# Scan layer: the B, C and x tiles of groups 1 to 3 projected with 512-column matmuls and a later sum

## The chip, the cores and the metric

The kernel runs on one core of a Trainium2 chip. A core has a matrix engine (TensorE, "PE" in the profile, with "PEld" for its weight loads), a vector engine (VectorE, "DVE"), an activation engine (ScalarE, "ACT"), GpSimd ("POOL") and SyncE ("SP"), which here only issues weight loads. The engines run side by side; each takes its own instructions strictly in the order in which the program wrote them, and waits for others through semaphores. Matmul results land in PSUM, a small memory of eight banks of 128 x 512 fp32 values; everything else is in SBUF.

The metric is the device time of one execution, in microseconds (us). Lower is better.

## What is computed

A trunk of two layers on 256 tokens of 1024 features. Each layer is a gated feed-forward block, a token mixer, and another feed-forward block, each followed by a layer norm. The mixer of layer 0 is a sparse attention, that of layer 1 a Mamba-2 scan. The change is in the scan only:

```python
def ssd_mixer(x, w_in, conv_w, conv_b, ...):
    z, xbc, dt = jnp.split(x @ w_in, [SSM_INNER, SSM_INNER + SSM_CONV_DIM], axis=-1)
    conv = conv_b + xbc_pad[:, 0:seq] * conv_w[0]          # 4 taps along the tokens
    for k in range(1, SSM_CONV):
        conv = conv + xbc_pad[:, k:k + seq] * conv_w[k]
    xs, b_in, c_in = jnp.split(jax.nn.silu(conv), ...)
    ...                                                    # dt, decay, chunked scan of 2 x 128 tokens
    yz = y.reshape(...) * jax.nn.silu(z)                   # gate, norm per group, norm_g
    return yz @ w_out
```

There are 4 groups of 512 channels of x (and of z), and one B and one C tile of 128 channels for each group.

## The kernel before

**Products in three parts.** fp32 accuracy is reached by splitting each weight tile and each activation into a high half H and a low half L; a product is H·H + H·L + L·H, three matmuls (`mm3`, L555 to L557). The weights stream in as *units* of 128 x 1024 values. SyncE loads a unit ("raw"), ScalarE casts it to its high half (`make`, L349, tile `wh`), VectorE subtracts to get the low half (`lows`, L378, tile `wl`). For six units of the scan (`by_dma`) ScalarE writes the negated high half (L355) and a GpSimd DMA adds the raw values (L356) instead. There are ten slots of `wh`/`wl`; `W.pump(n)` first does the low halves that are due, then casts up to n further units into slots that have come free.

**Projection of a B, C or x tile.** `proj_b` (L703) takes one weight unit, 128 output channels, and multiplies it with both halves of the transposed activations `xT`. The tile `xT.HL` holds, for each of 8 slices of the features, 256 columns of high halves and then 256 columns of low halves. Per slice there are three matmuls of 256 columns, 24 for a tile. `proj_w` (L712), used by the feed-forward blocks, does the same sum in another form: 8 matmuls of H with all 512 columns of `xT.HL` into a whole PSUM bank, then 8 matmuls of L with the 256 high columns, added to the first half of the bank. The two halves of the bank then have to be added: in the feed-forward blocks ScalarE copies one half out (L962) and VectorE adds the other (L963).

**The convolution.** `conv` (L1550) takes a projected tile in PSUM: ScalarE makes tap 3 and the bias (L1552), VectorE adds the three other taps (L1555), each on top of the one before, and the SiLU on ScalarE (L1547) is put off to the next tile (`late`, `flush`).

**Order of the scan's front.** Eight `bc_tile`s (four of B, four of C), with `cumsums` (sums of dt·a, needed by the decay; from there a 32 KB DMA to `scr` and the loads `decay_load` on the GpSimd queue) after tile 5; then the four x tiles of group 0, with the products C·B of all groups (`cb`, `cb_cross`, L1581 and L1573) after the second; then z of group 1, and the transposes `x_tok` of group 0. Each tile's projection goes to one of three PSUM banks in turn (`xbank`, tile `pxs`).

**The loop over groups.** For group g the list `f` holds eight pieces of TensorE work that fill the gaps of the scan's chain: for g = 0 and 1 the four x tiles of group g + 1 and four half tiles of z (`z_half`); for g = 2 the x tiles of group 3 between pieces of the output projection. Between the pieces stand, in this order: `f[0]`, `x_tok`, `f[1]`, `f[2]`, `diag(0)` and `gate(0)`, `f[3]`, `square(0)`/`root(0)`, `carry`, `diag(1)`, `gate(1)`, `norm(0)`, `f[4]`, `square(1)`/`root(1)`, `decay_seg`, `f[5]`, `y_tr(0)` (L1666), `norm(1)` (L1661), `f[6]`, `y_tr(1)`, `decay_exp`, `f[7]`. `gate` is VectorE (L1649, L1650), `square` ScalarE (L1654), `root` VectorE (L1657) and a GpSimd power (L547), `norm` ScalarE, and `y_tr` needs `norm`.

## Time and profile before

| | us |
|---|---|
| median of 3 runs | 1013.47 (1013.46 to 1014.56) |
| the profiled execution | 1013.54 |
| its span, from first to last instruction | 1011.8 |

The profile is of one execution; the span leaves 1.7 us of its time outside. The views used are: the page (busy time of each engine; the chain of work that ended last), the table of stretches (per stretch: its length, then busy us and count for PE, PEld, DVE, ACT and POOL, then granted clock of TensorE, share of the DMA engines, GB/s), the groups of instructions by line and shape (`xcount | busy us, mean ns of one | idle before`), the waits (who waited for whom: us in total, times, longest) and the timeline (start, duration, engine, line, operation, output<-inputs, form, xcount, and in brackets the idle time before and what ended it). Instructions in a row overlap at their ends, so the cost of one in a queue is the distance from its start to the start of the next.

### The profile page before, as it was taken

How to read it: one execution, taken by the hardware profiler on the slowest of the kernel's cores; microseconds unless marked ns; L12 is line 12 of the kernel's file. 1: busy time of each engine (PE TensorE's matmuls, PEld its weight loads, DVE VectorE, ACT ScalarE, POOL GpSimd, SP SyncE). 2: the span in 40 equal slices, each digit the busy share in tenths (PEclk: the TensorE clock that was granted, in tenths of full speed). 3: DMA queues.
4: the chain of work that ended last, by engine and by line, in shares of the span. 5: the costliest groups of instructions: out<-in, count | busy, mean ns of one | idle time of the engine just before them, and what ended most of it. 6: DMA issues, size and time to landing. Idle time of an engine off the chain costs nothing.

```text
span 1011.8 us, 14601 instructions
## 1 busy us (share of the span) xinstructions
PE 1000.9 (99%) x5279; PEld 847.7 (84%) x5279; DVE 913.8 (90%) x1294; ACT 657.8 (65%) x950; POOL 106.1 (10%) x153
## 2 busy tenths in 40 slices
PE   9999999999999999999999999999999999999996
PEld 7888888898788888888888888999889888888885
DVE  6999998789799999988999997787899899999985
ACT  6676775476657676754767675486876546776670
POOL 0101110200001110000111000151110101010000
PEclk9999999999999999999999999999999999999999
DMA  9979899352547999792899978347875554999751
GB/s 341 283 241 299 291 259 345 121 171 81 199 135 203 263 295 266 260 336 83 222 252 294 274 251 306 132 148 229 226 229 201 194 212 120 296 293 292 204 189 42
DMA packets 64664, 229.60 MB, mean 227 GB/s; under 512 B 7280, under 2 KB 8112, under 8 KB 64592
## 3 DMA queue, kind: packets, MB, share of 16 engines
q1 hardware_dynamic: 52128, 183.95, 50.8%
q0 software_dynamic: 12464, 44.72, 21.8%
q8 instruction: 41, 0.67, 0.3%
q14 instruction: 31, 0.25, 0.1%
HBM read 193.48 MB, written 1.08 MB: 192 GB/s over the span
## 4 chain that ended last, share of the span: by engine, by line
PE 95%; POOL 1%; DVE 1%; ACT 1%; DMA 1%; SPq 0%; issue 0%; DVEq 0%; POOLq 0%
PE pmm L557 13%; PE pmm L556 13%; PE pmm L555 13%; PE acc L555 10%; PE acc L556 10%; PE acc L557 10%; PE ptr L556 3%; PE ptr L557 3%; PE ptr L555 3%; PE pmm L717 2%; PE ptr L820 1%; PE ptr L1638 1%; PE pxs L555 1%; PE pxs L556 1%; PE pxs L557 1%; PE ptr L717 1%
## 5 line engine op out<-in xcount | busy, mean ns | idle before, releaser
L349 ACT CAST wh<-raw 128x1024 fp32r<-128x1024 f32 (+2 forms) x431 | 429.6, 1043 | 117.5 <-DVE raw L316 80.7
L378 DVE TENSOR_TENSOR wl<-raw,wh 128x1024 fp32r<-128x1024 f32 x421 | 493.3, 1212 | 11.1 <-ACT wh L349 11.1
L555 PE MATMUL acc<-wh,hH 128*128 128x512 f32 (+1 forms) x352 | 137.9, 392 | 0.0
L556 PE MATMUL acc<-wl,hH 128*128 128x512 f32 (+1 forms) x352 | 136.6, 388 | 0.0
L557 PE MATMUL acc<-wh,hL 128*128 128x512 f32 (+1 forms) x352 | 136.6, 388 | 0.0
L555 PE MATMUL pmm<-wh,xT 128*128 128x512 f32 (+2 forms) x320 | 126.0, 394 | 0.1
L556 PE MATMUL pmm<-wl,xT 128*128 128x512 f32 (+2 forms) x320 | 123.6, 386 | 0.4 <-DVE wl L378 0.4
L557 PE MATMUL pmm<-wh,xT 128*128 128x512 f32 (+2 forms) x320 | 123.5, 386 | 0.0
L289 POOL DMA_DIRECT2D raw<-raw x59 | 50.7, 866 | 401.7 <-DVE raw L316 216.5
L555 PE MATMUL pmm<-wh,xf 128*128 128x512 f32 x224 | 87.9, 392 | 0.0
L557 PE MATMUL pmm<-wh,xf 128*128 128x512 f32 x224 | 87.3, 390 | 0.0
L556 PE MATMUL pmm<-wl,xf 128*128 128x512 f32 x224 | 87.2, 389 | 0.0
L316 DVE TENSOR_TENSOR raw<-raw,raw 128x1024 f32<-128x1024 f32 x69 | 82.8, 1218 | 0.4
L557 PEld LDWEIGHTS acc<-wh,hL 128*128 128x128 f32 x352 | 66.1, 188 | 13.6
L556 PEld LDWEIGHTS acc<-wl,hH 128*128 128x128 f32 x352 | 66.2, 188 | 13.4 <-DVE wl L378 0.5
L555 PEld LDWEIGHTS acc<-wh,hH 128*128 128x128 f32 x352 | 66.2, 188 | 12.8
L556 PEld LDWEIGHTS pmm<-wl,xT 128*128 128x128 f32 x320 | 60.5, 189 | 12.9 <-DVE wl L378 1.5
L557 PEld LDWEIGHTS pmm<-wh,xT 128*128 128x128 f32 x320 | 60.2, 188 | 12.8 <-DVE xT L552 1.0
L555 PEld LDWEIGHTS pmm<-wh,xT 128*128 128x128 f32 x320 | 60.4, 189 | 11.1 <-ACT wh L349 0.5
L557 PEld LDWEIGHTS pmm<-wh,xf 128*128 128x128 f32 x224 | 42.0, 188 | 8.8
L555 PEld LDWEIGHTS pmm<-wh,xf 128*128 128x128 f32 x224 | 42.0, 188 | 8.6
L556 PEld LDWEIGHTS pmm<-wl,xf 128*128 128x128 f32 x224 | 42.1, 188 | 8.5
(332 smaller groups left out, 1821.3 us busy)
## 6 DMA issues: line engine op xcount, KB each, us to landing
raw<-in_wts_dram SPq DMA_DIRECT2D x338, 512.0 KB, 5.4
raw<-raw POOLq DMA_DIRECT2D x59, 512.0 KB, 6.1
M<-scr POOLq DMA_DIRECT2D x8, 512.0 KB, 6.2
lng<-in_ln_g_dram POOLq DMA_DIRECT2D x6, 512.0 KB, 6.3
lnb<-in_ln_b_dram POOLq DMA_DIRECT2D x6, 512.0 KB, 5.1
wl<-raw POOLq DMA_DIRECT2D x6, 512.0 KB, 5.9
raw<-in_wts_dram SPq DMA_DIRECT2D x4, 408.0 KB, 7.6
raw<-in_wts_dram SPq DMA_DIRECT2D x4, 256.0 KB, 3.9
```

Of the source, the lines that this page charges most:

```text
L289: self.nc.gpsimd.dma_start(self.raw[r], self.raw[other], accum_op=ALU.add)
L316: self.nc.vector.tensor_add(self.raw[r], self.raw[r], self.raw[other])
L349: nc.scalar.copy(h[:, c:c + n], raw[:, c:c + n])
L378: self.nc.vector.tensor_sub(lo[:, s], raw[:, s], h[:, s].bitcast(F32))
L555: nc.tensor.matmul(ps, lh, rh, start=first, stop=False, skip_group_check=on)
L556: nc.tensor.matmul(ps, lh, rl, start=False, stop=False, skip_group_check=on)
L557: nc.tensor.matmul(ps, ll, rh, start=False, stop=last, skip_group_check=on)
L717: nc.tensor.matmul(ps, H[:, k * 128:(k + 1) * 128], xT.HL[:, k, :], start=k == 0, stop=False)
L820: nc.tensor.transpose(pt[:, i * 256 + t * 128:i * 256 + (t + 1) * 128], h[:, i * 128:(i + 1) * 128], ident)
L1638: nc.tensor.matmul(py[:, h * 64:(h + 1) * 64], m[:, h * 128:(h + 1) * 128], y[t][:, h * 64:(h + 1) * 64], start=True, stop=True)
```

## The change

The B and C tiles and the x tiles of groups 0 to 2 (the title counts them 1 to 3) no longer go through `proj_b` and `conv` but through a new `conv_tile`; the x tiles of group 3 stay. That is 8 + 12 = 20 tiles.

```diff
-    def proj_w(ps, xT, u):
+    def proj_w(ps, xT, u, retire=True):
...
+        halves, taps = [], []
+        def conv_sum():
+            for ps, v, i, out_t in halves:
+                a = f1("cv")
+                nc.vector.tensor_add(v, ps[:, :SEQ], v)
+                nc.scalar.activation(a, v, AF.Identity, bias=convp_sb[:, 4, i:i + 1], scale=convp_sb[:, 3, i:i + 1])
+                taps.append((v, a, i, out_t))
+            halves.clear()
+            flush()
+        def conv_taps():
+            for v, a, i, out_t in taps:
+                for s in range(1, 4):
+                    nc.vector.scalar_tensor_tensor(a[:, s:], v[:, :SEQ - s], convp_sb[:, 3 - s, i:i + 1], a[:, s:],
+                                                   op0=ALU.mult, op1=ALU.add)
+                late.append((out_t, a))
+            taps.clear()
+        def conv_tile(uu, i, out_t, n, bank):
+            conv_sum()
+            ps = bank()
+            proj_w(ps, xT, uu, False)
+            W.free(uu)
+            v = f1("cs")
+            nc.scalar.copy(v, ps[:, SEQ:])
+            W.pump(n)
+            conv_taps()
+            halves.append((ps, v, i, out_t))
...
-            if i == 5:
+            if i == 6:
                 cumsums()
...
+        conv_sum()
         z_half(1, 1, 0, uz)
+        conv_taps()
         decay_seg(0, 0)
         flush()
...
-                f += [lambda t=t, i=i: (z_half(g + 2, t, i, u + 4), W.pump(1)) for t in range(2) for i in range(2)]
+                f += [lambda t=t, i=i: (conv_sum(), z_half(g + 2, t, i, u + 4), W.pump(1), conv_taps())
+                      for t in range(2) for i in range(2)]
```

So tile n's two halves are summed at the start of tile n + 1 (`conv_sum`), its taps are written at the end of tile n + 1 behind that tile's `W.pump` (`conv_taps`), and its SiLU comes at the start of tile n + 2. The queues per tile n are then: TensorE 8 matmuls of 512 and 8 of 256 columns; VectorE the sum of tile n − 1, the low halves that are due, the taps of tile n − 1; ScalarE the first tap of tile n − 1, the SiLU of tile n − 2, the copy of tile n, the casts. The first tap and the other three now read SBUF instead of PSUM. `cumsums` moves behind tile 6. For g = 0 and 1 the sum and the taps of the last x tile fall into `f[4]`, that is behind `gate(1)`.

## The prediction

> **What bounds the kernel now.** I read the page's busy shares and its chain first, then the stretch that holds all 20 changed tiles.

> ```profile
> PE 1000.9 (99%) x5279; PEld 847.7 (84%) x5279; DVE 913.8 (90%) x1294; ACT 657.8 (65%) x950; POOL 106.1 (10%) x153
> ...
> PE 95%; POOL 1%; DVE 1%; ACT 1%; DMA 1%; SPq 0%; issue 0%; DVEq 0%; POOLq 0%
> ```
> ```profile
> 656.50:746.00 89.50, 89.36 (x674) 84.62 (x674) 75.75 (x142) 70.36 (x103) 22.00 (x35) 1.00 0.68 199
> ```

> The chain is TensorE almost alone, and in this stretch TensorE stands still for 0.14 of 89.5 us. VectorE is busy for 75.75, which looks like room for a little more. That share is a mean, though, and both queues run in written order, so the question is which wait a longer VectorE queue would make.

> **What goes: TensorE time.** Timeline, three tiles in a row in the old form up to the next work, then one feed-forward tile in the new form:

> ```profile
> 702.05 0.36 PE L555 MATMUL pxs<-xT,wh 128*128 128x256 f32 x1
> ...
> 710.76 1.90 PE L1638 MATMUL ptr<-xdt,M 128*128 128x64 f32 x16
> ```
> ```profile
> 978.15 1.98 PE L717 MATMUL ptr<-xT,wh 128*128 128x512 f32 x8
> ...
> 980.91 2.00 PE L717 MATMUL ptr<-xT,wh 128*128 128x512 f32 x8
> ```
> ```profile
> PEld ptr L1475 <- POOL adt L1467: 0.3, 1, 0.3
> ```

> Old: 8.71 us less 0.08 for the first matmul behind transposes, over three, is 2.88 a tile. New: 2.76. The columns streamed are the same (8 x 512 + 8 x 256 = 24 x 256); what goes is a fixed part of eight matmuls. 20 x 0.117 = **2.3 us** less. The wait of `cumsums` for GpSimd goes too, **0.3**, as it moves one tile back. [...]

> **What is added: prices in the two queues.** VectorE and ScalarE, timeline; the rows at 618 are the feed-forward copy (L962) and sum (L963), the same operations in the same shape; the last row is from the groups.

> ```profile
> 660.83 1.16 DVE L378 TENSOR_TENSOR wl<-raw,wh 128x1024 fp32r<-128x1024 f32 x1
> 662.37 1.52 DVE L1555 SCALAR_TENSOR_TENSOR cv<-pxs,convp_sb,cv 128x255 f32<-128x255 f32 x3 [0.38 <-ACT cv L1552]
> 663.80 2.48 DVE L378 TENSOR_TENSOR wl<-raw,wh 128x1024 fp32r<-128x1024 f32 x2
> 666.21 1.50 DVE L1555 SCALAR_TENSOR_TENSOR cv<-pxs,convp_sb,cv 128x255 f32<-128x255 f32 x3
> 667.63 1.23 DVE L378 TENSOR_TENSOR wl<-raw,wh 128x1024 fp32r<-128x1024 f32 x1
> 668.78 1.50 DVE L1555 SCALAR_TENSOR_TENSOR cv<-pxs,convp_sb,cv 128x255 f32<-128x255 f32 x3
> ```
> ```profile
> 618.82 0.42 DVE L963 TENSOR_TENSOR h<-ptr,h 128x256 f32<-128x256 f32 x1 [0.90 <-ACT h L962]
> 619.16 1.22 DVE L378 TENSOR_TENSOR wl<-raw,wh 128x1024 fp32r<-128x1024 f32 x1
> ```
> ```profile
> 618.42 0.37 ACT L962 COPY h<-ptr 128x256 f32<-128x256 f32 x1 [1.16 <-PE ptr L719]
> 618.68 0.42 ACT L973 ACTIVATE gate<-gate 128x256 f32<-128x256 f32 x1
> 619.00 1.04 ACT L349 CAST wh<-raw 128x1024 fp32r<-128x1024 f32 x1
> ```
> ```profile
> 661.78 0.56 ACT L1552 ACTIVATE cv<-pxs,convp_sb 128x256 f32<-128x256 f32 x1
> 662.24 1.04 ACT L349 CAST wh<-raw 128x1024 fp32r<-128x1024 f32 x1
> 663.17 0.56 ACT L1552 ACTIVATE cv<-pxs,convp_sb 128x256 f32<-128x256 f32 x1
> 663.97 1.28 ACT L1547 ACT_TABLE_LOAD   x1 [0.23 <-DVE cv L1555]
> ```
> ```profile
> L675 DVE SCALAR_TENSOR_TENSOR x<-x,rs,lnb 128x256 f32<-128x256 f32 x2 | 0.9, 480 | 0.0
> ```

> Start to next start: taps 1.43, a low half 1.14, the new sum 0.34; first tap 0.46, cast 0.94, the new copy 0.26, SiLU 0.32, table load 1.29. The copy waits for the whole tile (L719), not only for the 512-column part. The taps read SBUF in future: L675, the same operation from SBUF, takes 480 ns, the taps (1.50 for three) as much, so I take no gain; the other end is a plain two-input pass at the new sum's 0.34 each, 1.02 for three.

> So a tile costs VectorE 1.14 + 1.43 = 2.57 before, and 2.91 after, while TensorE's 2.88 becomes 2.76. **VectorE was the faster and becomes the slower of the two**, and nothing waits for that until the first consumer does.

> **Step 1: the wait at `cb`.** The last old taps of the C tiles, ScalarE's low-half product, the last C SiLU, and `cb`:

> ```profile
> 682.64 1.52 DVE L1555 SCALAR_TENSOR_TENSOR cv<-pxs,convp_sb,cv 128x255 f32<-128x255 f32 x3 [0.45 <-ACT cv L1552]
> ```
> ```profile
> 683.88 1.06 ACT L355 ACTIVATE wl<-wh 128x1024 fp32r<-128x1024 f32 x1
> ...
> 685.29 0.40 ACT L1547 ACTIVATE cTt<-cv 128x256 f32<-128x256 f32 x1
> ```
> ```profile
> 687.35 0.83 PE L1581 MATMUL psp<-cTt,bT 128*128 128x128 f32 x6
> ```
> ```profile
> 656.58 0.28 PE L555 MATMUL pxs<-xT,wh 128*128 128x256 f32 x1
> ```

> In the trace VectorE starts 2.9 us late (tile 0's matmuls end at 659.5, its taps start at 662.37), catches up at 0.3 a tile and by 682.64 waits itself; the SiLU is done 1.7 us ahead of `cb`. After: VectorE is free at 662.0 and has the two low halves first, so the sum of tile 0 starts at 664.3, 4.9 late. Six tiles of 2.91 take it to 681.7, 0.7 more where ScalarE's first table load stands ahead of a copy, 0.6 for the copies of `cumsums`, 2.91 for tile 6 and 0.34 for the sum of tile 7: 686.3. Its taps need ScalarE, which from 682.0 on has two table loads for the Exp of `cumsums` and back (2.6), a first tap, a SiLU, a copy, a cast and that L355 product (0.46 + 0.32 + 0.26 + 0.94 + 1.0), two small Exps (0.2) and the first tap of tile 7 (0.56): 688.3. Then taps 1.43, the next tile's sum 0.42, its first tap 0.46, and the SiLU of tile 7, 0.42: **691.1** for `cb`. TensorE comes there at 656.58 + 10 x 2.76 + 1.7 (`cumsums`) = 685.9, and 0.9 later as tile 6 needs the PSUM bank of tile 3, whose sum ends at 674.1 when TensorE is ready at 673.2. Wait: 0.9 + 4.3 = **5.2 us**. Behind it on TensorE stand two x tiles and z. If ScalarE only ever delayed VectorE by the first tap of tile 7, the end would be 688.9 and the wait 3.0; with the taps at 1.02 it is about 3.0 too, as ScalarE's part stays.

> **Step 2: the wait at `y_tr(1)`, twice.** Group 0: end of `diag(1)`, `gate`, root, square, norm, transpose; then the norm and transpose of group 1:

> ```profile
> 717.99 0.48 PE L555 MATMUL pmm<-wh,xT 128*128 128x512 f32 x1
> ...
> 726.74 0.60 PE L1666 MATMUL ptr<-ident,xdt 128*128 128x128 f32 x4
> ```
> ```profile
> 721.34 0.69 DVE L1649 TENSOR_TENSOR xdt<-ptr,xtok 128x512 f32<-128x512 f32 x1
> ...
> 723.55 0.15 DVE L1657 TENSOR_SCALAR ss<-ss 128x1 f32<-128x1 f32 x1 [0.79 <-ACT xtok L1654]
> ```
> ```profile
> 722.79 0.63 ACT L1654 ACTIVATE xtok<-xdt 128x512 f32<-128x512 f32 x1 [0.53 <-DVE xdt L1650]
> ...
> 725.65 0.73 ACT L1661 ACTIVATE xdt<-xdt,rs 128x512 f32<-128x512 f32 x1
> ...
> 754.47 0.73 ACT L1661 ACTIVATE xdt<-xdt,rs 128x512 f32<-128x512 f32 x1
> ```
> ```profile
> 755.43 0.60 PE L1666 MATMUL ptr<-ident,xdt 128*128 128x128 f32 x4
> ```
> ```profile
> 707.59 1.52 DVE L1555 SCALAR_TENSOR_TENSOR cv<-pxs,convp_sb,cv 128x255 f32<-128x255 f32 x3 [0.45 <-ACT cv L1552]
> ```

> The norm ends 0.36 us ahead of the transpose in group 0 (725.65 + 0.73, 726.74) and 0.23 in group 1: hardly any room. VectorE reaches `gate(1)` 3.35 us after `diag(1)` ends (717.99, 721.34).

> After, ahead of `gate(1)`: three sums are added (1.0); a wait of 0.7 where a sum and a first tap follow each other and that tile's unit is one of the GpSimd ones, so that no low half stands between; a wait of 1.3 at `root(0)`, since `square(0)` now stands on ScalarE behind the copy of x tile 3, a cast and an L355 product (0.26 + 0.94 + 1.0). The taps of x tile 3 move behind `gate(1)` (−1.4), and the 0.45 of idle time at 707.59 goes. That is 1.1, and TensorE's shorter tiles bring it there 0.3 earlier: 1.4 later than now. Behind `gate(1)`, the last x tile's sum (0.42), its first tap (0.46), the SiLU of the tile ahead (0.33) and a cast (0.94) now stand before `square(1)`, the taps before `root(1)`, and one more SiLU (0.33) before the norm: 2.5, less the 0.53 for which ScalarE idled at 722.79: 2.0. In group 0 that makes 1.4 + 2.0 − 0.36 = **3.0**, in group 1, in the same order with 0.23 of room, **3.2**; two pieces of z and the next x tile are queued behind it. The x tiles of group 3 are unchanged and I add nothing there. Bounds: 0 if VectorE's idle time takes it all, 4 each. With taps at 1.02, 2.3 each.

> **Costed at nothing:** the `scr` write and decay loads on GpSimd's queue move some 4 us, and needed at 698 in the trace, at 703 by the walk, they landed by 692 and would by 696; SP's loads are tied to the low halves, whose units run six tiles ahead of their use.

> **Sum**: −2.3 − 0.3 + 5.2 + 3.0 + 3.2 = **+8.8 us** on the profiled 1013.54: **1022.3**. The median shown is 0.07 below that.

> **Rivals.**
> (a) *TensorE stays the only bound*: the queues swallow 0.34 a tile, and only 2.6 go: 1010.9. For it: 14 us of idle VectorE in the stretch, and that no row of PE waits there before. Against: step 1 is a sum of work in one queue, and a wait at `cb` vanishes only if VectorE's tile costs under about 2.3. Chance 0.13. Waits of just 2.6 in all give no change, 1013.5: 0.06.
> (b) *One of the two places only*, the other absorbed: +2.6 (`cb` alone) or +3.6 (the transposes alone), 1016.1 to 1017.1, and all three at part of their size up to +7, 1020.5: 0.20.
> (c) *Taps get cheaper in SBUF*: at 1.02 a tile the waits left are 3.0 + 2 x 2.3, less 2.6: +5.0, 1018.5. Against it stands L675. Chance 0.08. [...]
> (d) *The clock falls* while TensorE stands at `cb`:

> ```profile
> 1003.00:1004.00 1.00, 0.17 (x2) 0.00 (x0) 0.76 (x2) 0.00 (x0) 0.00 (x0) 1.00 0.00 0
> ...
> 1007.00:1008.00 1.00, 0.00 (x0) 0.00 (x0) 0.35 (x1) 0.00 (x0) 0.00 (x0) 0.79 0.58 219
> ```

> In the tail the granted clock goes to half 4.4 us after the last matmul (0.79 is 0.58 full and 0.42 half). A wait of 4.3 just misses that; if it hits, and as long a time runs at half speed, 2.2 more: 1024.5, chance 0.05. [...]
> The forecast itself, +7 to +10.5: 0.48.

> **Range.** 1015 to 1025 holds the forecast, (b), (c) and (d), 0.81. A measurement of this kernel tells about 0.2%, 2 us, from no change: faster 0.13, same 0.06, slower 0.81.

> **What would show it.** Right: TensorE waits for `cTt` of ScalarE at `cb` by 3 to 5 us and for the norm at L1666 twice by 2 to 4; L717 rows at 2.76 a tile; VectorE without idle time from tile 0 to `cb`. Wrong: no wait at `cb`, or taps well under 1.4 a tile.

## The result and the profile after

The changed kernel takes **1028.72 us** in the median of 4 runs (1027.09 to 1029.75), the kernel before 1013.92 beside it: a ratio of 1.0144, interval 1.0132 to 1.0156, or 14.8 us more. The prediction was 1022.3 with 1025 as its upper end. The direction was right, the size too small.

The page of the profiled execution (1028.65, span 1026.9): busy shares, then shares of the chain.

```profile
PE 1004.7 (98%) x5119; PEld 842.6 (82%) x5119; DVE 921.8 (90%) x1314; ACT 664.4 (65%) x970; POOL 108.1 (11%) x153
...
PE 87%; DVE 6%; ACT 4%; issue 1%; DMA 1%; SPq 0%; DVEq 0%; ACTq 0%
```

TensorE has 160 matmuls fewer for the same columns and is *longer* busy, 1004.7 instead of 1000.9; a slower clock is one thing that would do that. And VectorE and ScalarE, 1% each in the chain before, now hold 6% and 4%. The waits of TensorE in the scan (who waited for whom: us in total, times, longest) name the places:

```profile
PE ptr L1696 <- ACT xdt L1691: 6.6, 2, 3.4
PE psp L1611 <- ACT cTt L1548: 3.9, 2, 2.0
PE pxs L717 <- DVE cs L1556: 0.8, 2, 0.5
```

L1696 is `y_tr`, L1691 the norm, L1611 `cb`, L1548 the SiLU, L1556 the new sum. These are the waits that the prediction forecast. Timeline of the front, first tiles in a row, then tiles later on, and the sums of VectorE that free their banks:

```profile
656.62 1.99 PE L717 MATMUL pxs<-xT,wh 128*128 128x512 f32 x8
...
662.20 2.00 PE L717 MATMUL pxs<-xT,wh 128*128 128x512 f32 x8
...
671.02 2.11 PE L717 MATMUL pxs<-xT,wh 128*128 128x512 f32 x8
...
674.54 2.11 PE L717 MATMUL pxs<-xT,wh 128*128 128x512 f32 x8 [0.46 <-DVE cs L1556]
```
```profile
670.55 0.42 DVE L1556 TENSOR_TENSOR cs<-pxs,cs 128x256 f32<-128x256 f32 x1
...
674.07 0.42 DVE L1556 TENSOR_TENSOR cs<-pxs,cs 128x256 f32<-128x256 f32 x1
```

Two tiles from 656.62 to 662.20: 2.79 each. The fifth to the seventh tile each start some 0.05 us behind the sum that frees their bank (671.02 after 670.55 + 0.42, 674.54 after 674.07 + 0.42), and the tenth 0.14 behind its own: there TensorE goes at VectorE's pace, 3.52 for the tile at 671.02. The view of waits counts from the recorded end of the matmul before, which in a row overlaps the next start (671.00 for the tile at 671.02), so its 0.8 is less than what the waits cost.

Then `cb`, TensorE and below it the three rows that make it late:

```profile
688.00 0.61 PE L1611 MATMUL psp<-cTt,bT 128*128 128x128 f32 x4
690.52 0.49 PE L1611 MATMUL psp<-cTt,bT 128*128 128x128 f32 x2 [1.91 <-ACT cTt L1548]
693.04 0.79 PE L1611 MATMUL psp<-cTt,bT 128*128 128x128 f32 x2 [2.04 <-ACT cTt L1548]
693.63 1.92 PE L1611 MATMUL pmm<-cTt,bT 128*128 128x128 f32 x8
...
696.90 2.82 PE L717 MATMUL pxs<-xT,wh 128*128 128x512 f32 x8
```
```profile
684.07 0.41 DVE L1482 COPY at<-ptr 32x256 f32<-32x256 f32 x1 [1.22 <-ACT eacs L1480]
...
690.19 1.52 DVE L1565 SCALAR_TENSOR_TENSOR cv<-cs,convp_sb,cv 128x255 f32<-128x255 f32 x3 [2.10 <-ACT cv L1557]
```
```profile
692.59 0.40 ACT L1548 ACTIVATE cTt<-cv 128x256 f32<-128x256 f32 x1
```

The last SiLU of C ends at 692.99 and the last two matmuls start at 693.04. But look at the durations behind: eight small matmuls take 1.92 (1.06 in a kernel further down), and the x tile's wide part 2.82 instead of 2.00. The clock is slow there, as the table of stretches shows (length, busy us and count of PE, PEld, DVE, ACT, POOL, then the **granted clock**, share of the DMA engines, GB/s). In slices of 0.2 us the clock changes within 691.60 to 691.80 (mean 0.61), 698.40 to 698.60 (0.82), 770.00 to 770.20 (0.88) and 773.40 to 773.60 (0.59). Between 1.00 and 0.50 on either side that is a fall at 691.64 and a rise at 698.47, 6.83 later, and a fall at 770.15 and a rise at 773.56, 3.41 later. The two falls are 78.51 us apart, 23 times 3.413, so the stretches are laid 3.413 us apart, to meet these four:

```profile
688.23:691.64 3.41, 0.87 (x6) 0.49 (x4) 1.38 (x4) 3.38 (x6) 1.23 (x2) 1.00 0.90 267
691.64:695.06 3.42, 2.02 (x9) 2.02 (x10) 3.35 (x7) 2.13 (x5) 0.00 (x0) 0.50 1.03 220
695.06:698.47 3.41, 3.41 (x15) 3.12 (x14) 2.37 (x5) 1.18 (x3) 0.00 (x0) 0.50 0.38 79
698.47:701.88 3.41, 3.41 (x20) 2.96 (x19) 1.81 (x4) 1.37 (x3) 0.00 (x0) 1.00 0.81 312
732.60:736.02 3.42, 1.50 (x7) 0.92 (x5) 3.01 (x12) 3.42 (x8) 0.56 (x1) 1.00 0.82 287
736.02:739.43 3.41, 2.19 (x12) 1.89 (x13) 3.41 (x12) 3.38 (x6) 0.00 (x0) 1.00 0.71 226
766.74:770.15 3.41, 0.91 (x6) 0.87 (x7) 3.41 (x12) 3.41 (x6) 0.03 (x1) 1.00 0.53 181
770.15:773.56 3.41, 3.41 (x9) 2.64 (x9) 3.41 (x8) 3.38 (x4) 0.00 (x0) 0.50 0.43 142
```

The clock is at one half for two such stretches behind the wait of `cb` and for one behind the second wait of `y_tr(1)`, and stays up behind the first:

```profile
737.25 0.66 PE L1696 MATMUL ptr<-ident,xdt 128*128 128x128 f32 x4 [3.15 <-ACT xdt L1691]
```
```profile
769.24 0.66 PE L1696 MATMUL ptr<-ident,xdt 128*128 128x128 f32 x4 [3.43 <-ACT xdt L1691]
```

So theory 1: the two longer queues make the forecast waits of 10.5 us, and the idle TensorE loses its clock in them, which costs some 4 us more. Rivals: the tile form costs something at each tile; the waits cost only themselves; the delay by one piece, or VectorE's load, is the whole cause.

### The profile page after: what moved, and what is told of

It reads as the page before. It is cut to its first block, busy times and chain, and to the rows that moved or that the text cites. A ratio compares the mean times of both kernels' runs of the same rounds, so it can differ in the third digit from the quotient of the medians.

```text
span 1026.9 us, 14303 instructions
## 1 busy us (share of the span) xinstructions
PE 1004.7 (98%) x5119; PEld 842.6 (82%) x5119; DVE 921.8 (90%) x1314; ACT 664.4 (65%) x970; POOL 108.1 (11%) x153
## 4 chain that ended last, share of the span: by engine, by line
PE 87%; DVE 6%; ACT 4%; issue 1%; DMA 1%; SPq 0%; DVEq 0%; ACTq 0%
PE pmm L557 12%; PE pmm L556 12%; PE pmm L555 12%; PE acc L555 10%; PE acc L557 10%; PE acc L556 10%; PE ptr L556 3%; PE ptr L557 3%; PE ptr L555 3%; PE pmm L717 2%; DVE wl L378 1%; ACT wh L349 1%; PE ptr L821 1%; DVE cv L1565 1%; PE ptr L717 1%
## 5 line engine op out<-in xcount | busy, mean ns | idle before, releaser
L349 ACT CAST wh<-raw 128x1024 fp32r<-128x1024 f32 (+2 forms) x431 | 430.3, 1043 | 117.1 <-DVE raw L316 80.2
L378 DVE TENSOR_TENSOR wl<-raw,wh 128x1024 fp32r<-128x1024 f32 x421 | 493.8, 1214 | 12.2 <-ACT wh L349 11.7
L555 PE MATMUL acc<-wh,hH 128*128 128x512 f32 (+1 forms) x352 | 138.0, 392 | 0.0
L555 PE MATMUL pmm<-wh,xT 128*128 128x512 f32 (+2 forms) x320 | 126.3, 395 | 0.1
L555 PE MATMUL pmm<-wh,xf 128*128 128x512 f32 x224 | 87.9, 392 | 0.0
L556 PEld LDWEIGHTS acc<-wl,hH 128*128 128x128 f32 x352 | 66.2, 188 | 13.4 <-DVE wl L378 0.4
L555 PEld LDWEIGHTS acc<-wh,hH 128*128 128x128 f32 x352 | 66.2, 188 | 12.9
L555 PEld LDWEIGHTS pmm<-wh,xT 128*128 128x128 f32 x320 | 60.7, 190 | 11.3 <-ACT wh L349 0.5
L555 PEld LDWEIGHTS pmm<-wh,xf 128*128 128x128 f32 x224 | 42.1, 188 | 8.6
```

The source lines that it names most:

```text
L349: nc.scalar.copy(h[:, c:c + n], raw[:, c:c + n])
L378: self.nc.vector.tensor_sub(lo[:, s], raw[:, s], h[:, s].bitcast(F32))
L555: nc.tensor.matmul(ps, lh, rh, start=first, stop=False, skip_group_check=on)
L556: nc.tensor.matmul(ps, lh, rl, start=False, stop=False, skip_group_check=on)
```

## The experiments

Each kernel is the changed one with the edit shown, if not said otherwise; ratios are to the kernel before, run beside it (1013.6 to 1014.3).

**Half of the tiles at a time.** First B, C and group 0 only, then groups 1 and 2 only.

```diff
-            if g < 3:
+            if not g:
                 conv_tile(uu, g * 4 + i, o, 1, xbank)
...
-                f += [lambda t=t, i=i: (conv_sum(), z_half(g + 2, t, i, u + 4), W.pump(1), conv_taps())
-                      for t in range(2) for i in range(2)]
+                f += [lambda t=t, i=i: (z_half(g + 2, t, i, u + 4), W.pump(1)) for t in range(2) for i in range(2)]
```

The second has `0 < g < 3` there, keeps that list as in the change, and has B, C and `cumsums` as before.

> Only the eight B and C tiles and the four x tiles of group 0 have the new form (cumsums one tile later, as in the change); the x tiles of groups 1 and 2 and the z pieces beside them are those of before. Theory (the added VectorE work makes a lag that cb and y_tr(1) run into, and each longer wait also halves the TensorE clock for some microseconds): the wait of cb stays near 4 us and the clock falls to about a half after it; the two waits of y_tr(1) are gone. In the trace of the change x_tok(0,0) came 7.5 us later than before, so 1013.9 + 7.5 = about 1021.4, range 1020 to 1022.5. Rival (the tile form itself costs, the same at each tile): 12 of 20 tiles carry 12/20 of the 14.8 us, 1022.8, and cb has no large part of it. Rival (waits alone, no clock): 1013.9 + 3.5 to 4.5 = 1017.4 to 1018.4.

> Only the eight x tiles of groups 1 and 2 have the new form, with the sum and taps of the last of them beside the z piece; B, C and group 0 and the place of the cumsums are those of before. Theory: cb waits as before (no new wait); y_tr(1) waits 3.2 and 3.4 us in groups 0 and 1 (minus 8 x 0.085 for the tiles: +5.9), and a clock that falls after one or both waits adds 0 to 1.7 each: 1013.9 + 5.9 + 1.7 = 1021.5, range 1019.8 to 1023.2. Rival (the tile form itself costs the same at each tile): 8 of 20 of 14.8 = 1019.8, without 3 us waits at y_tr(1). Rival (the waits at y_tr(1) are left over from the lag at cb): no waits there, 1013.2.

Front only: 1021.05, ratio 1.0067 (1.0054 to 1.0079). Groups only: 1020.79, 1.0063 (1.0050 to 1.0075). The waits of TensorE there, front only and groups only:

```profile
PE psp L1611 <- ACT cTt L1548: 3.9, 2, 2.0
```
```profile
PE ptr L1700 <- ACT xdt L1695: 6.6, 2, 3.4
```
```profile
763.00:765.00 2.00, 2.00 (x6) 1.52 (x6) 2.00 (x6) 1.97 (x3) 0.00 (x0) 0.50 0.52 197
```

The last row is the clock in groups only, behind its second wait. Each half keeps its own waits at the same size, and 7.2 + 6.9 make 14.1 of the 14.8. The eight tiles of the groups cost as much as the twelve of the front, so a fixed price of the form at each tile does not fit, and the waits at `y_tr(1)` are no remains of the lag at `cb`.

**The same twenty tiles without the delay.** Copy, sum, first tap and late taps at the tile itself:

```diff
-            conv_sum()
             ps = bank()
...
             nc.scalar.copy(v, ps[:, SEQ:])
+            halves.append((ps, v, i, out_t))
+            conv_sum()
+            conv_taps()
             W.pump(n)
-            conv_taps()
-            halves.append((ps, v, i, out_t))
```

> All twenty tiles keep the 512-column form and the sum, but copy, sum, first tap and late taps are issued at the tile itself, not one piece later. Theory (the load of VectorE is what lags, and the delay by one piece hides part of the chain copy, sum, first tap): each tile's chain now stands in a row, so VectorE idles within it and lags more: cb waits 7.4 us, y_tr(0) 3.5 and 2.6, diag 0.7, bank waits near 0.9 each; +17.9 without the clock, and with clock periods like those of the change (3 to 6 us) +21 to +24: about 1036, range 1031 to 1039. Rival (the delay by one piece is what makes the chains late, not the load): the silu of the last C tiles comes earlier, cb waits as before, and the time is below the change's 1028.7, near 1014 to 1020.

1034.12, 1.0200 (1.0186 to 1.0214), inside the theory's range; the wait at `cb` is 6.5, not 7.4. VectorE now stands still inside each tile, and `cb` waits longer:

```profile
668.30 1.52 DVE L1565 SCALAR_TENSOR_TENSOR cv<-cs,convp_sb,cv 128x255 f32<-128x255 f32 x3 [0.67 <-ACT cv L1557]
```
```profile
PE psp L1611 <- ACT cTt L1548: 6.5, 2, 3.3
```

VectorE waits for the first tap at all 20 tiles there, 13.4 us in total (0.67 each); in the change it does so at seven, 7.6 us in total. Given the sum, the delay by one piece is the better of the two orders.

**What does the clock cost?** The waits are filled with transposes that do nothing for the output.

```diff
+        def fill(pt, n):
+            for _ in range(n):
+                nc.tensor.transpose(pt[:, :128], ident, ident)
         def y_tr(t, g):
             pt = ptr()
+            if t and g < 2:
+                fill(pt, 36)
...
+                fill(ptr(), 46)
                 cb(0)
```

> The change with the waits filled: 46 fp32 transposes of the identity (0.0875 us each, 4.0 us) on TensorE ahead of cb, into a bank that nobody reads, and 36 (3.15 us) ahead of the transposes of y_tr(1) in groups 0 and 1, into its own bank. They do no work for the output and end about when the wait would. Theory (the waits stay, but the idle TensorE lost its clock): the granted clock stays at 1.00 in 690 to 700 and 765 to 775, the pieces after the waits run at their normal length, and some 4 to 5 us come back: 1028.7 - 4.5 = 1024.2, range 1023 to 1026. Rival (the clock falls by the time or by what follows, not by the idle of TensorE; or the slow pieces are slow for another reason): 1028.7 or up to 1 us more.

> As e4_busy, with fills cut to the waits: one fp32 transpose took 0.109 us there, so the fills ran past the waits by some 0.6 us at each place. Now 39 ahead of cb (4.25 us) and 29 and 31 ahead of y_tr(1) (3.2 and 3.4 us). Theory (the clock that falls in the waits costs what the trace of the change shows after them: 1.95 between cb and the next x tile, 0.78 in that tile, 1.66 after the second y_tr(1), 4.4 in all): 1028.7 - 4.4 = 1024.3, range 1023.3 to 1025.3. Rival (what e4_busy gave back, 2.4, is all that the clock costs): 1026.3.

The first try gave 1026.35, 1.0119 (1.0106 to 1.0133), less than expected: 46 transposes took from 688.90 to 693.92, 5.02 us, 0.109 each and not 0.0875 (four of `y_tr` in the change's trace: 0.35, from 796.38 to what follows at 796.73), so they ran past the waits.

```profile
688.90 5.18 PE L1695 MATMUL ptr<-ident 128*128 128x128 f32 x46
...
693.92 1.06 PE L1611 MATMUL psp<-cTt,bT 128*128 128x128 f32 x8
```

With shorter fills (39, 29 and 31): 1024.65, 1.0108 (1.0094 to 1.0123), within 0.4 of the forecast. Stretches of that run over the three places:

```profile
688.00:700.00 12.00, 12.00 (x91) 11.24 (x91) 8.99 (x17) 9.07 (x16) 1.64 (x3) 1.00 0.70 186
732.00:736.00 4.00, 4.00 (x35) 3.68 (x33) 3.90 (x14) 3.97 (x8) 0.56 (x1) 1.00 0.90 277
765.00:774.00 9.00, 8.96 (x67) 8.21 (x66) 8.91 (x18) 8.94 (x11) 0.00 (x0) 1.00 0.51 192
```

The clock is 1.00 throughout. The results that TensorE needs come no sooner, no work is less, and 1028.72 − 1024.65 = **4.1 us** come back: that is the clock's part. (Against the kernel before beside each it is 14.8 − 11.0 = 3.8; in the two traces the way from the first tile's first matmul to the first `acc`, the output projection, takes 124.08 and 119.93, 4.15 less.)

**Load or order?** The sum lengthens VectorE's queue, and sum, taps and SiLU each stand a piece later. Three kernels take them apart: the change with one tap less; the kernel before with an addition more; the order of the change with the tiles of before.

```diff
-                for s in range(1, 4):
+                for s in range(1, 3):
```

> The change without the last of the three late taps on its twenty tiles (that product is left out of the convolution). VectorE has 0.48 us less per tile: 1.43 to 0.95, so 2.43 a tile in all instead of 2.91, below TensorE's 2.79. Theory A (VectorE's load alone makes the lag): the bank waits and the waits of cb and y_tr(1) are gone: 1013.9 less 20 x 0.085 for the tiles, less some 0.3 for the cumsums: about 1012, range 1011 to 1013.5. Theory B (the load makes a part, the order with sum, first tap and late taps a piece later makes the rest): cb still waits 2.6 us and y_tr(1) 2.2 us twice, no bank waits, and waits this short mostly keep the clock: +4.75, 1018.6, range 1017.5 to 1020.5.

1021.15, 1.0079 (1.0066 to 1.0091): above theory B's range, far from A's. The waits are near B's at `cb`, 3.1 for its 2.6, with none for a bank; at `y_tr(1)` they are 2.1 and 0.6 instead of 2.2 twice:

```profile
PE psp L1611 <- ACT cTt L1548: 3.1, 2, 1.5
PE ptr L1696 <- ACT xdt L1691: 2.7, 2, 2.1
```
```profile
689.46:692.87 3.41, 1.57 (x11) 1.38 (x12) 3.17 (x6) 3.41 (x7) 0.67 (x1) 1.00 1.00 246
692.87:696.28 3.41, 3.41 (x15) 3.12 (x14) 2.98 (x6) 1.28 (x4) 0.00 (x0) 0.50 0.68 144
...
730.43:733.84 3.41, 1.44 (x7) 0.86 (x5) 2.70 (x10) 3.41 (x9) 0.56 (x1) 1.00 0.77 256
733.84:737.25 3.41, 3.27 (x10) 2.79 (x11) 3.41 (x12) 3.36 (x5) 0.89 (x1) 0.50 0.66 241
```

My "mostly keep the clock" was wrong: stretches in which TensorE was busy for 1.57 and 1.44 of 3.41 us were followed by one at half the clock in this execution. The six runs go from 1019.54 to 1024.83, a spread of 5.3 us; the kernel before has 1.6 in 17 runs.

```diff
             flush()
+            if not 12 <= i < 16:
+                nc.vector.tensor_add(f1("cj"), ps[:, :SEQ], a)
```

> The kernel before, with one more VectorE addition per tile on the same twenty tiles, ahead of the late taps: the tile's 256 columns in PSUM plus the conv output into a scratch tile that nobody reads, 0.34 us, the size of the change's sum. The order, the tile form and ScalarE are those of before. Theory (of the change's lag the load makes the smaller part and the order, a piece later, the larger): no wait at cb, y_tr(1) waits 0.7 and 1.2 us, a bank wait of 0.2; about +2: 1015.7, range 1014.6 to 1017. Rival (the load of VectorE alone, 2.91 us a tile against 2.8 to 2.9, makes the waits of the change): cb waits 4 us and y_tr(1) 3 us twice: 1023 or more.

1018.72, 1.0048 (1.0036 to 1.0061), above my range of 1014.6 to 1017, but without the change's waits:

```profile
PE ptr L1668 <- ACT xdt L1663: 2.3, 2, 1.4
PE pxs L555 <- DVE cv L1557: 0.6, 1, 0.6
```

Of the 5.0 us, 1.4 lie ahead of the stage in this trace, in code that is the same: the first tile starts at 657.96 instead of 656.58. From there to the first `acc` it takes 112.46 us instead of 108.67, 3.8 more, and 2.9 of these are the waits above.

```diff
-            proj_w(ps, xT, uu, False)
+            proj_b(ps[:, :SEQ], xT, uu, False)
             W.free(uu)
-            v = f1("cs")
-            nc.scalar.copy(v, ps[:, SEQ:])
...
-                nc.vector.tensor_add(v, ps[:, :SEQ], v)
```

> The order of the change without its sum and copy: the twenty tiles are multiplied in the form of before (three matmuls a slice into 256 columns), but first tap and late taps are issued one piece later, as in the change, and read PSUM. VectorE and ScalarE have the work of before. Theory (order and load each make a part, together more than their sum, since the one uses up the slack that the other needs): cb waits 1.1, y_tr(1) 1.1 and 1.3, +3.0: 1016.7, range 1015.5 to 1018.5, with the clock mostly kept by waits this short. Rival A (the order is harmless): 1013.2. Rival B (the order alone makes the change's waits): cb 4 us, y_tr(1) 3 us twice, 1023 or more.

1015.65, 1.0025 (1.0015 to 1.0034): inside the range, but by luck, as the place was wrong. `cb` does not wait; the delayed taps hold the PSUM bank, and TensorE waits for that:

```profile
PE pxs L555 <- DVE cv L1564: 1.9, 1, 1.9
```

Load alone costs 5.0 (3.8 in the stage), order alone 1.9, and the change, which has both, 14.8, or 11.0 at a full clock. That each uses up slack that the other would need fits this, but is not shown: the change also has a copy on ScalarE and shorter tiles on TensorE, and no run has these alone.

**Where the readers stand.** `cb` one tile later, first in the change, then with the front's twelve tiles only:

```diff
-            if i == 1:
+            if i == 2:
                 cb(0)
```

> The change with cb(0), cb(1) and cb_cross behind the third x tile of group 0 instead of the second. Theory (VectorE and ScalarE are late by a fixed lag, not by something that cb triggers): the wait of cb falls from 4 us to about 1.5, x_tok(0,0) waits 0.4, the clock stays up at the front, and the waits of y_tr(1) and the fall after one of them stay: 1013.9 + 7.2 + 1.7 = 1022.8, range 1021 to 1024.5. Rival (the wait comes with cb wherever it stands, since its own silu is late by the order): 4 us of wait behind the third tile, clock at a half there, about 1028.

> As e1_front (the new form in the B, C and group 0 tiles only), with cb(0), cb(1) and cb_cross behind the third x tile of group 0 instead of the second. The twelve tiles and all their work are the same as in e1_front; only the place of the reader differs. Theory: cb waits about 1.3 us instead of 4, x_tok(0,0) some 0.5, the clock stays at 1.00, and +1.1 is left: 1014.8, range 1014 to 1016 (e1_front: 1021.05). Rival (the twelve tiles cost it): as e1_front, 1020 to 1021.

1023.56, 1.0097 (1.0084 to 1.0110), and 1017.36, 1.0029 (1.0017 to 1.0041). Moving one reader past the lag gave back some 5 and 4 us, with all work kept. The first landed as forecast; its waits at `cb` and `y_tr(1)`, and the stretch of the first wait at `y_tr(1)`, 3.40 us here, with the one behind it:

```profile
PE ptr L1696 <- ACT xdt L1691: 5.3, 2, 3.4
PE psp L1611 <- ACT cTt L1548: 1.2, 1, 1.2
```
```profile
730.47:733.88 3.41, 0.16 (x1) 0.16 (x2) 3.07 (x12) 3.41 (x8) 0.56 (x1) 1.00 0.82 299
733.88:737.29 3.41, 3.41 (x11) 2.83 (x11) 3.41 (x11) 3.36 (x4) 0.89 (x1) 0.51 0.56 192
```

The second missed by 2.6: I had the bank waits 1 us too small again, and `x_tok(0,0)` waited 0.8 instead of 0.5; the rest is open. It lies between the theory and its rival, and is no gain over the kernel before.

**Can any of it be kept?** The four x tiles of group 0 only (with `cumsums` one tile later); and the front with GpSimd making the sum (with `cb` one tile later).

> Only the four x tiles of group 0 have the new form; B, C and groups 1 and 2 are those of before, the cumsums stand behind the seventh tile as in the change. Theory: nothing reads these four tiles within two pieces of 2.8 us, so no wait comes: 4 x 0.085 less, and about 0.5 less for the wait of the cumsums: 1013.9 - 0.8 = 1013.1, range 1012.4 to 1013.8. Rival (the form costs the same at each tile): 4 of 20 of 14.8: 1016.9.

1013.66 in 11 runs, 0.9998 (0.9989 to 1.0007): no difference. In the trace the stage itself is shorter. Its first matmul and its first `x_tok`, and below that the `x_tok` of the kernel before, whose first matmul is at 656.58:

```profile
657.92 0.28 PE L555 MATMUL pxs<-xT,wh 128*128 128x256 f32 x1
...
701.86 0.27 PE L1659 MATMUL pxt<-ident,xsT 128*128 128x128 f32 x1
```
```profile
701.26 0.27 PE L1625 MATMUL pxt<-ident,xsT 128*128 128x128 f32 x1
```

43.94 instead of 44.68 us, 0.74 less, as forecast; but this execution came to the stage 1.3 us later, in code that is the same. So this trace has the gain in the stage, but it is smaller than what the stages ahead vary by.

```diff
-                nc.vector.tensor_add(v, ps[:, :SEQ], v)
...
-            v = f1("cs")
-            nc.scalar.copy(v, ps[:, SEQ:])
+            c, v = f2("ch"), f1("cs")
+            nc.scalar.copy(c, ps)
+            nc.gpsimd.tensor_add(v, c[:, :SEQ], c[:, SEQ:])
```

> As e12_front_cb2, with the sum taken from VectorE: ScalarE copies all 512 columns to SBUF (some 0.2 us more than the copy of 256) and GpSimd adds the halves there, at the tile itself. VectorE has the work per tile of before. Theory (without the sum VectorE keeps up): the bank waits go, as the copy frees the bank, cb waits 0.2 us or not at all: 12 x 0.085 less and 0.5 less for the cumsums: 1012.3, range 1011.5 to 1013.5. No trace here has a GpSimd addition of this size; 128x64 took 0.3 to 0.5 us there, so about 1 to 2 us is to be expected; under 2.8 us a tile it keeps up, but it stands in the chain ahead of the first tap. Rival (its own lateness takes the sum's place): cb waits 1 to 2 us: 1013.5 to 1015.

1022.99, 1.0086 (1.0072 to 1.0100), a clear miss. The addition takes 0.72 in the row below (0.85 in the mean of the twelve), but its queue was occupied:

```profile
675.61 3.78 PE L717 MATMUL pxs<-xT,wh 128*128 128x512 f32 x8 [6.34 <-ACT ch L1577]
```
```profile
673.73 0.72 POOL L1578 TENSOR_TENSOR cs<-ch 128x256 f32<-128x256 f32 x1
```

GpSimd works on dt for `cumsums` until 673.7, so the first sum waits for that, though the copy that it needs ended at 663.71, and ScalarE, VectorE and TensorE stood behind it. I had asked what one addition costs and not what stands ahead of it.

## Why the prediction was too low, point by point

- **The step that failed is the sum.** It held the waits and gave the clock no term: "−2.3 − 0.3 + 5.2 + 3.0 + 3.2 = +8.8". The fall of the clock stood among the rivals at 0.05, at `cb` only, "a wait of 4.3 just misses that". That rival is what came true, at 4.1 instead of its 2.2 and at a second place besides `cb`. It belonged to the forecast: the longest wait that goes without a fall here is 3.15 us, waits of 1.91 and 2.04 with two matmuls between them made one, and the fills show what the falls cost, 4.1 us. The reason for the low chance was the one fall in the trace of before, 4.4 us after the last matmul. I read that distance as a threshold; it is only one case of it. With the clock's 4.1, 1.1 for the bank waits and 0.6 for the tiles (the points below), the forecast of +8.8 becomes +14.6; the other waits together came out as forecast, and 14.8 was measured.
- **What decides is the place of the wait, too.** In the stretches above, those of 3.41 us that were busy for 0.87 and 0.91 (and, with one tap less, 1.44 and 1.57) are followed by half the clock; those busy for 1.50 and 2.19 are not, though a wait of 3.15 lay across them. The border is near 1.5 and not sharp in these figures: 1.57 fell and 1.50 did not. With `cb` one tile later, the first wait of `y_tr(1)` lay within one stretch, busy for 0.16, and the clock fell there. A stretch busy for 2.02 at half the clock did not end it, the full one behind it did (3.41, up to the rise at 698.47). The times at half the clock, 6.83 and 3.41, and the 78.51 us between the two falls, 691.64 and 770.15, are 2, 1 and 23 times 3.413: that fits a fixed grid, and more than the fit was not shown. A stretch busy for 1.57 of 3.41, 46%, was still followed by a fall. So a wait of over 3 us cost nothing more in one place (3.15) and, as an estimate, 1.7 in another (3.43, with 3.41 us at half the clock behind it), and its length alone does not give the number.
- **Bank waits: 0.9 predicted, 2.0 measured.** From 656.62 to 688.00 are 31.38 us; ten tiles of 2.79 and 1.49 of `cumsums` are 29.4. The walk had the right mechanism at tile 6 alone; in the trace the sums set the pace from the fifth tile to the seventh and again at the tenth.
- **Tiles: −2.3 predicted, −1.7 measured** (20 x 0.085): 2.79 in a row, not the 2.76 of the feed-forward tile.
- **The wait at `cb`: 4.3 predicted, 3.95 measured**, at a later time than I had it. The copies of `cumsums` on VectorE waited 1.22 us for ScalarE's Exps behind a table load of 1.28, which I had priced on ScalarE's queue only; the 2.10 us of VectorE waiting for the first tap was foreseen as 2.0 (686.3 to 688.3).
- **`y_tr(1)`: 3.0 and 3.2 predicted, 3.15 and 3.43 measured.** Right, in both places and for the reason given: VectorE reaches `gate(1)` of group 0 1.6 us later than before (4.92 behind `diag(1)` instead of 3.35; forecast 1.4), and from there to the norm it takes 2.05 more (forecast 2.0).
- **Rival (c) is out**: the taps take as long from SBUF, 480 ns in the row below, as from PSUM, 477 for the same shape in the kernel before.

```profile
L1565 DVE SCALAR_TENSOR_TENSOR cv<-cs,convp_sb,cv 128x255 f32<-128x255 f32 x20 | 9.6, 480 | 7.6 <-ACT cv L1557 7.6
```

- **Rivals (a) and (b) are out**: both places wait, and each costs about 7 us with its own clock periods. Without the clock the change stands at 1024.65, 2.4 above the forecast, near the upper end of the range.

What stays open: in the kernels whose waits lie between 2 and 3.4 us I saw the clock in one execution each; that the spread of their times comes from where the waits lie on the grid of 3.413 us fits the traces, but was not shown run by run; up to 1.4 us of a spread can lie ahead of the stage, where the first tile starts at 656.58 to 657.96 in the fourteen traces. Why load alone cost 3.8 in its stage and not 2 was not taken apart beyond the waits shown.

## What to carry to other kernels

When a change lets TensorE wait for some 2 us or more within 3.4, put a second term beside the wait: here the clock ran at 0.50 for 6.83 us behind waits of 1.91 and 2.04 and for 3.41 behind one of 3.43, stayed at 1.00 behind one of 3.15, and the work that follows paid 4.1 us. When a step moves 0.1 us from TensorE to a queue that is nearly as long, walk that queue up to its first reader; what counts is how soon TensorE needs something that stands behind the added work (the four tiles that nobody reads for two pieces cost nothing, the eight ahead of `gate` and the norm cost 7 us). And before work is given to an idle engine, look at what its queue holds at that time, not at its share of the span.
